# Output tiles one block behind the chain instead of two, and the sample tile in the fifth block

## The chip, the cores and the metric

One Trainium2 chip, one of its cores. A core has TensorE (PE; PEld is its loading of weights), VectorE (DVE), ScalarE (ACT), GpSimd (POOL) and SyncE (SP, which here issues most transfers), each with its own queue of instructions, and 16 DMA engines. The metric is the device time of one execution in microseconds (us).

## The reference

One step of a decoder layer for a prompt of 2048 tokens and a group of 64 sample tokens, with the same weights, 1024 wide:

```python
h = rms_norm(x, norm_pre)
proj = jnp.einsum('btd,de->bte', h, w_in)
...
oc, new_shift, new_S = rwkv7_mix(pc, shift_prev, wkv_S, ...)
...
o = jnp.concatenate([oa, ob, oc, od], axis=-1) * jax.nn.silu(gate)
y = x + rms_norm(jnp.einsum('bte,ed->btd', o, w_out), norm_post)
```

Four groups of heads share the 1024 columns: attention (oa), a gated linear recurrence (ob), RWKV-7 time mixing (oc) and a state space (od). Group C, the RWKV mixing, is a recurrence over the tokens: for each token, `S = S * w + (S @ -kk) (kk * a) + v k` and `y = S r`, for 4 heads with a 64 x 64 state each.

## The kernel before, in words

The input projection, the attention and the groups B and D run first. The last stage, from about 1200 us on, is group C and with it the output projection. Group C goes through the prompt in 16 blocks of 128 tokens, each of two halves of 64 (`rw_prompt`). A block i has these parts:

- the **front** of block i + 2 (`rw_prep`, `rw_mats`, `rw_base`): it depends on the projection alone, not on the state. `rw_prep` makes r_kk, r_W and r_F out of r_X; `rw_mats` multiplies W by F on PE (`ra<-r_W,r_F`), masks the products into r_W and r_ET, and ends with the reduction r_de (L1214). r_de is written to memory (zd) and read back spread out (r_zr); `rw_base` then solves 16 x 16 triangles on VectorE, in 15 pairs of a product (L1262, r_x16w) and a sum (L1263, r_x). The first of them is the row of 128x60 elements;
- **tri** (`rw_tri`): it makes TT of the 16 x 16 inverses by four small products on PE (`rl<-...`);
- the **chain** (`rw_chain`), the recurrence itself, for each half: W times Z on PE, then TT times gs (`rc<-r_gs,r_TT`), which ACT copies into Q, a part of the tile r_Z; BK times Q (`rc<-r_Z,r_BK`), from which VectorE makes the next state (r_Z, L1372); ET times Q (`rc<-r_Z,r_ET`), which ACT copies to r_y;
- the **norm** (`rw_norm`): r_nm, r_yc, r_nss, an inverse square root in small steps (r_nrs), a turn on PE (`rl<-ident,r_yc`), r_yo; and at its end `out_prep`, which multiplies by the gate (o_o), finds a scale by way of o_mx, a 128x1 product on PE (L1550) and the small rows o_q and o_sc, and writes the two halves of o_h (L1561 on ACT, L1562 on VectorE).

`out_tile` is the output projection of 128 tokens: 2 x 24 matmuls of 128 x 512 (L1584), the norm (o_ss, o_y) and the sum with x (o_x, on POOL), which SP stores. There are 16 tiles of the prompt and tile 16 with the 64 sample tokens. A tile's matmuls are laid into the chain of a block: `spine` holds that chain's PE steps, and the k-th group of three matmuls may not start before its share of the steps (`issue_after`). What the loop at L1864 decides is in which block a tile goes out: at block i, tile t goes out if t is at most i - LAG - 1, and LAG is 1. So tile i - 2 is laid into the chain of block i. Tile 16 is prepared in block 15 (`out_prep(16)`) and goes out after tile 14, ahead of tile 15.

The order of the instructions on each engine is then set by a scheduler, which goes through the program with a model of the engines and puts on each what it holds to be ready. An engine works through its order and waits where an operand is missing. Of the pools, o_h and o_x have two buffers, and r_zr has one.

Of the kernel before, what the change touches and what calls it, by code (L numbers as in the profile page):

```python
# [1754 lines left out]
def weave(gens):  # L1755

    gens = [[g, 0, n] for g, n in gens]
    while any(x[2] > 0 for x in gens):
        g = min(gens, key=lambda x: x[1] / abs(x[2]))
        step = next(g[0], 0)  # L1760
        g[1] += 1 if step is None else step
        if step == 0:
            gens.remove(g)


def drain(gen):
    for _ in gen:
        pass


def program(tc, ins, outs):
    with ExitStack() as ctx:
        p = Part(ctx, tc, ins, outs)
        pool = lambda st, name, **kw: st.enter_context(tc.tile_pool(name=name, bufs=1, reuse_waits="tile", **kw))
        nc = tc.nc
        p.attn_consts()
        ph2 = ctx.enter_context(ExitStack())
        with ExitStack() as ph1:
            hp = pool(ph1, "hp", side="right")
            acc = p.pwp = pool(ph1, "acc", space=PSUM, side="right")  # L1780

            def paced(cols, lead):
                pos = -lead
                p.anchors = []

                def after(n):
                    nonlocal pos
                    pos += n
                    i = int(pos * len(p.anchors) / (cols + 1))
                    return p.anchors[min(i, len(p.anchors) - 1)] if pos > 0 else None  # L1790

                return after

            kps = ctx.enter_context(ExitStack())
            kp, sac = pool(kps, "s5k"), pool(kps, "sac")
            with ExitStack() as va:
                vp = pool(va, "vp")
                p.w16b, p.w32b = 8, W32B
                with ExitStack() as st:
                    wp, ps = pool(st, "wp"), pool(st, "stp", space=PSUM)  # L1800
                    lps = pool(st, "lgp", space=PSUM, side="right")
                    sp = wp
                    lr = pool(st, "lr")
                    p.norm_consts(sp)
                    p.wqkv = {0: p.load_w(0, wp, True)}
                    p.norm_in(0, hp, sp, ps)
                    x0, h0 = p.xt_dma, p.hfs[-1]
                    p.qkv_start(wp, vp)
                    for k, b in enumerate(BORD):
                        if k < 4:  # L1810
                            p.norm_in(BORD[k + 1], hp, sp, ps)
                            x1, h1 = p.xt_dma, p.hfs[-1]
                        p.qk(b, sp, acc)
                        with tc.issue_after(x0), tc.issue_after(h0):
                            if k == 0:
                                p.lam_consts(sp, ps)
                                p.lru_consts(sp, ps)
                                p.lru_start(lr)
                            if k == 1:
                                p.proj_dram()  # L1820
                                p.s5_consts(kp, sp)
                            if b == 4:
                                p.sample_consts(sac)
                        if k or LV:
                            p.lru(b, lr, lps, acc)
                        p.vtokens(b, sp, acc)
                        if k == 0 and not LV:
                            p.lru(b, lr, lps, acc)
                        x0, h0 = x1, h1
                p.w16b, p.w32b = W16B, W32C  # L1830
                ev, wp = pool(ph1, "ev", side="right"), pool(ph1, "wp2", side="right")
                aside = p.wo_steps(wp)
                with ExitStack() as st:
                    at, ps = pool(st, "at"), pool(st, "atp", space=PSUM)
                    after = paced(len(FILL) * 2 * TT, LEAD)
                    drain(p.attn_prompt(at, ps))
                    drain(p.proj_rest(FILL, wp, ev, acc, after, aside))
        with kps, ExitStack() as st:
            sp, ps = pool(st, "sa"), pool(st, "sap", space=PSUM)
            weave([(p.attn_sample(sp, ps), SW), (p.s5(pool(st, "s5"), pool(st, "xps", space=PSUM)), S5N)])  # L1840
        with ph2:
            rw, p.late = pool(ph2, "rw", side="right"), pool(ph2, "rwl", side="right")
            p.rps, p.rpb = pool(ph2, "rp", space=PSUM, side="right"), {"ra": 2, "rl": 2, "rc": 2}
            op = pool(ph2, "op")
            with ExitStack() as st:
                p.rwkv_consts(rw)
                seq = p.rw_prompt(rw)
                weave([(p.s5_glu(pool(st, "s5g"), pool(st, "xg", space=PSUM)), 8), (islice(seq, 2 + 4 * RB), RBW)])
            ops = pool(ph2, "ops", space=PSUM)
            p.out_consts(op)  # L1850
            p.opool = pool(ph2, "ot")
            sm = pool(ph2, "sm")
            p.rwkv_sample_consts(sm)
            smp = p.rw_sample(rw, sm)

            def out(t, spine=()):
                if t not in p.prep:
                    p.out_prep(t)
                if GA and t + 1 < 15 and t + 1 not in p.gated and t + 1 not in p.prep:
                    p.out_gate(t + 1)  # L1860
                p.out_tile(t, *p.prep.pop(t), p.opool, ops, spine)

            t = 0
            for i in range(RB, 16):  # L1864
                mark = len(p.spine)
                n = min(-((t - 14) // (16 - i)), i - LAG - t)
                for k in range(4):
                    next(seq, 0)
                    if k in SK:
                        next(smp, 0)  # L1870
                    if n > 0 and k in POSL:
                        out(t, p.spine[mark:])
                        t, n, mark = t + 1, n - 1, len(p.spine)
                    if i == 15 and k == TK:
                        p.out_prep(16)
                while n > 0:
                    out(t)
                    t, n = t + 1, n - 1
            while t < 15:
                out(t)  # L1880
                t += 1
            out(16)
            out(15)


# [11 lines left out]
TK = 1  # L1897
# [21 lines left out]
XTB = 4  # L1919
W16B = 3  # L1920
SSB = 3
LAG = 1
ES = 999
RSP = ()
NAC = 0
# [55 lines left out]
```

## Time and profile before

| | |
|---|---|
| median of 3 runs | 1850.08 us (1841.87 to 1852.64) |
| profiled execution | 1846.33 us |
| its span, first to last instruction | 1844.5 us |
| PE, DVE, ACT, POOL busy | 81%, 79%, 49%, 44% |
| granted PE clock, mean of the span | 0.88 of full speed |

The span is what the profile covers; the profiled execution's own time lies 1.8 us above it. A row of a timeline gives start and duration in us, engine, line, operation, the tile written and those read, the shapes, a count where equal rows follow each other, and in brackets how long the engine stood idle before it and for whom.

### The profile page before, as it was taken

What the parts mean: (1) busy time and instruction counts of PE and PEld (TensorE: products, weight loads), DVE (VectorE), ACT (ScalarE), POOL (GpSimd) and SP (SyncE); (2) the same over time, 40 slices, a digit from 0 to 9 for tenths busy, and PEclk for the clock granted to TensorE, in tenths of its full rate; (3) what the DMA queues carried; (4) which work ended last, traced back from release to release, by engine and by line L of the source; (5) the groups of instructions that cost most, each with busy time, mean ns of one, the idle gap of its engine ahead of it and who ended that gap; (6) DMA issues with size and microseconds to landing.
All of it is one profiled execution on the core that took longest, in us unless ns stands there. A gap on an engine that the chain in (4) does not pass through costs nothing.

```text
span 1844.5 us, 33323 instructions
## 1 busy us (share of the span) xinstructions
PE 1497.3 (81%) x10956; PEld 844.9 (46%) x10956; DVE 1448.1 (79%) x4619; ACT 902.1 (49%) x2211; POOL 811.6 (44%) x887
## 2 busy tenths in 40 slices
PE   4889888987789788878894899657688887887887
PEld 2445644444344344434442456446455454554443
DVE  7797639988899899889896754376878887888865
ACT  3455746655556566657772222243344454444333
POOL 3441326736668877443344454261324333333312
PEclk9999998999899899989996999875777887887889
DMA  4422144575445655464447877635223233333221
GB/s 147 128 91 93 28 116 117 125 149 117 111 111 139 152 141 146 106 145 115 86 104 199 274 250 238 205 96 163 73 66 100 81 105 93 92 86 102 66 72 58
DMA packets 300898, 225.33 MB, mean 122 GB/s; under 512 B 192531, under 2 KB 248565, under 8 KB 300213
## 3 DMA queue, kind: packets, MB, share of 16 engines
q1 hardware_dynamic: 288388, 184.85, 37.4%
q10 hardware_dynamic: 8496, 24.76, 4.7%
q0 software_dynamic: 3840, 13.61, 2.6%
q8 instruction: 86, 1.41, 0.3%
q14 instruction: 88, 0.71, 0.1%
HBM read 130.04 MB, written 53.24 MB: 99 GB/s over the span
## 4 chain that ended last, share of the span: by engine, by line
DVE 34%; PE 21%; DMA 15%; issue 8%; POOL 4%; ACT 3%; SPq 1%; ACTq 0%; POOLq 0%; DVEq 0%
PE acc L206 7%; DMA r_zr<-zd 5%; DVE a_mx L365 4%; PE acc L1584 4%; DVE a_e L389 4%; DMA a_wt<-a_w 3%; DVE r_x L1263 2%; DVE r_x16w L1262 2%; DVE a_w L395 2%; DMA zd<-r_de 2%; PE ss L511 2%; DVE r_W L1177 1%; PE pf L530 1%; POOL a_e L388 1%; POOL a_w L395 1%
## 5 line engine op out<-in xcount | busy, mean ns | idle before, releaser
L206 PE MATMUL acc<-hT,w 128*128 128x512 f16 (+1 forms) x3120 | 633.6, 353 | 24.7 <-ACT pst L640 4.3
L206 PEld LDWEIGHTS <-w 128*128 128x128 f16 x3120 | 269.7, 101 | 322.3 <-issue 66.8
L368 ACT ACTIVATE a_e<-s,a_mx,sig 128x512 f32<-128x512 f32 (+3 forms) x320 | 226.9, 715 | 122.6 <-DVE a_mx L366 106.4
L1584 PE MATMUL acc<-wo,o_h 128*128 128x512 f16 (+1 forms) x816 | 225.1, 422 | 1.2 <-ACT o_y L1588 0.6
L365 DVE TENSOR_REDUCE a_mx<-s 128x1 f32<-128x512 f32 (+3 forms) x320 | 186.3, 599 | 23.4 <-PE s L361 18.7
L388 POOL TENSOR_SCALAR a_e<-a_e,a_al 128x512 f32<-128x512 f32 (+3 forms) x160 | 114.6, 731 | 148.6 <-DVE a_al L384 119.4
L389 DVE SCALAR_TENSOR_TENSOR a_e<-a_e,a_al 128x512 f32<-128x512 f32 (+3 forms) x160 | 149.3, 948 | 9.2 <-POOL a_e L388 9.0
L361 PE MATMUL s<-kh,qh 128*128 128x512 f16 (+3 forms) x320 | 105.7, 359 | 38.2 <-ACT a_e L368 35.0
L402 PE MATMUL pv<-vtok,a_wt 128*128 128x128 f16 x544 | 70.0, 230 | 64.6 <-DMA a_wt<-a_w 57.9
L392 ACT CAST a_w<-a_e 128x512 f16<-128x512 f32 (+3 forms) x160 | 86.3, 557 | 69.9 <-DVE a_e L389 63.5
L1584 PEld LDWEIGHTS <-o_h 128*128 128x128 f16 (+1 forms) x816 | 76.6, 105 | 95.1 <-issue 26.3
L395 POOL TENSOR_TENSOR a_w<-a_e,a_w 128x512 f16<-128x512 f32 (+3 forms) x80 | 90.0, 1128 | 64.4 <-ACT a_w L392 62.4
L1262 DVE TENSOR_TENSOR r_x16w<-r_zr,r_x 128x60 f32<-128x60 f32 (+18 forms) x255 | 58.8, 231 | 67.0 <-DMA r_zr<-zd 63.8
L1599 POOL TENSOR_TENSOR o_x<-o_y,o_x 128x512 f32<-128x512 f32 (+1 forms) x33 | 48.4, 1487 | 121.4 <-DVE o_y L1597 84.7
L402 PEld LDWEIGHTS <-a_wt 128*128 128x128 f16 x544 | 52.2, 104 | 91.4 <-DMA a_wt<-a_w 76.1
L395 DVE TENSOR_TENSOR a_w<-a_e,a_w 128x512 f16<-128x512 f32 (+2 forms) x80 | 76.9, 964 | 2.7 <-ACT a_w L392 2.7
L170 POOL TENSOR_TENSOR hT<-hf,hT 128x512 f16<-128x512 f32 (+1 forms) x36 | 36.5, 1022 | 88.3 <-ACT hT L168 88.2
L403 PE MATMUL pv<-vtok,a_wt 128*128 128x64 f16 x544 | 66.1, 202 | 0.0
L1263 DVE TENSOR_TENSOR r_x<-r_x,r_x16w 128x60 f32<-128x60 f32 (+18 forms) x255 | 62.4, 245 | 3.4
L368 ACT ACTIVATION_READ_ACCUMULATOR a_e<-s,a_mx,sig 128x1 f32 x320 | 64.0, 200 | 0.0
L366 DVE TENSOR_SCALAR a_mx<-a_mx,sig 128x1 f32<-128x1 f32 x320 | 59.8, 201 | 0.4
L511 PE MATMUL ss<-kv,qbd 128*32 128x256 f32 x256 | 52.5, 415 | 6.7 <-DMA kv<-in_ckv 6.5
(552 smaller groups left out, 3378.0 us busy)
## 6 DMA issues: line engine op xcount, KB each, us to landing
kv<-in_ckv SPq DMA_DIRECT2D x128, 256.0 KB
w<-in_w_in ACTq DMA_DIRECT2D x20, 512.0 KB
pc<-pst SPq DMA_DIRECT2D x40, 256.0 KB
xw<-in_xT SPq DMA_DIRECT2D x16, 512.0 KB
w<-in_w_out ACTq DMA_DIRECT2D x16, 512.0 KB
sg<-pst SPq DMA_DIRECT2D x32, 256.0 KB
r_X<-pc SPq DMA_DIRECT2D x16, 512.0 KB
r_zr<-zd SPq DMA_DIRECT2D x16, 512.0 KB
```

Of the source, the lines that this page charges most:

```text
L206: self.nc.tensor.matmul(acc[:, :n], w16[:, k, a, :], h[:, k, e, :], start=(c == 0), stop=(c == 3 * KT - 1))
L361: ins = nc.tensor.matmul(s[:, :kn], q[:, c], kh[:, c, k0:k0 + kn], start=True, stop=True)
L365: nc.vector.tensor_reduce(mx[:, p, c:c + 1], s[:, :kn], axis=AX.X, op=ALU.max, negate=True)
L368: nc.scalar.activation(e[:, :kn], s[:, :kn], AF.Exp, scale=sig, bias=mx[:, p, c:c + 1], accum_out=l[:, p, c:c + 1])
L388: nc.gpsimd.tensor_scalar(e1[:, :kn], e1[:, :kn], al[:, p, 1:2], 0.0, op0=ALU.mult, op1=ALU.add)
L389: nc.vector.scalar_tensor_tensor(e0[:, :kn], e0[:, :kn], al[:, p, 0:1], e1[:, :kn], op0=ALU.mult, op1=ALU.add)
L395: eng.tensor_tensor(w[:, kn:], e0[:, :kn], w[:, :kn], op=ALU.subtract)
L402: ins = nc.tensor.matmul(pv[:, :P], wt[:, j], v, start=kt == 0, stop=kt == qb, skip_group_check=True)
L511: ins = nc.tensor.matmul(sp[g:g + 32, 256 * j:min(256 * j + 256, n)], self.qbd[:, m, s].rearrange("p a q -> p (a q)"), rhs, start=True, st ...
L1262: XV.tensor_tensor(w[:, :, :m], zr[:, k, :, k + 1:], x[:, :, k:k + 1].to_broadcast([P, nu, m]), op=ALU.mult)
L1263: XV.tensor_tensor(x[:, :, k + 1:], x[:, :, k + 1:], w[:, :, :m], op=ALU.add)
L1584: nc.tensor.matmul(a[:n].rearrange("p (c n) -> p c n", c=4), h[:, k, e], self.wo[:, 4 * g:4 * g + 4, k, f, :], start=c == 0, stop=c == 3 * ...
```

## The change

LAG goes from 1 to 0, so tile t may go out in block t + 1: tile i - 1 is laid into the chain of block i. Tile 16 is no longer prepared in block 15 and put out at the end, but prepared and put out in block 4, after the second of the block's four parts. Tiles 14 and 15 stay behind the loop. The instructions of a tile are the same.

```diff
                     if n > 0 and k in POSL:
                         out(t, p.spine[mark:])
                         t, n, mark = t + 1, n - 1, len(p.spine)
-                    if i == 15 and k == TK:
-                        p.out_prep(16)
+                    if i == 4 and k == TK:
+                        out(16)
...
             while t < 15:
                 out(t)
                 t += 1
-            out(16)
             out(15)
...
-LAG = 1
+LAG = 0
```

PE's order in the second half of block 13, of the kernel before. `acc<-wo,o_h` are the output tile's matmuls, `rc` the chain's steps TT, BK and ET; "..." stands for further pairs of the two L1584 rows and, ahead of ET, for two rows of tri and the front and one of the next half.

```order
L44 MATMUL rc<-r_gs,r_TT 64x64 x4
L1584 LDWEIGHTS o_h
L1584 MATMUL acc<-wo,o_h 128x512
...
L44 MATMUL ra<-r_W,r_F 128x128 x8
L44 MATMUL rc<-r_Z,r_BK 64x64 x4
L1584 LDWEIGHTS o_h
L1584 MATMUL acc<-wo,o_h 128x512
...
L44 MATMUL rc<-r_Z,r_ET 64x64 x4
```

Three matmuls of an output tile stand there between TT and BK, and six between BK and ET. The same place on PE in the changed kernel:

```order
L44 MATMUL rc<-r_gs,r_TT 64x64 x4
L1584 LDWEIGHTS o_h
L1584 MATMUL acc<-wo,o_h 128x512
...
L44 MATMUL rc<-r_Z,r_BK 64x64 x4
L1584 LDWEIGHTS o_h
L1584 MATMUL acc<-wo,o_h 128x512
...
L44 MATMUL rc<-r_Z,r_ET 64x64 x4
L1584 LDWEIGHTS o_h
L1584 MATMUL acc<-wo,o_h 128x512
...
L44 MATMUL ra<-r_W,r_F 128x128 x8
```

Now 20 matmuls stand between TT and BK, 22 between BK and ET, and 4 between ET and the front's product W by F, which stood ahead of BK.

VectorE's order at the same place, around the state's row r_Z, in the kernel before:

```order
L1372 TENSOR_TENSOR r_Z<-rc,r_sd 64x128 x2
L1180 TENSOR_TENSOR r_F<-r_kka,r_Di 64x4x64 x2
L1262 TENSOR_TENSOR r_x16w<-r_zr,r_x_20691 128x4x4
L1263 TENSOR_TENSOR r_x_20691<-r_x_20691,r_x16w 128x4x4
L1409 TENSOR_REDUCE r_nm<-r_y 128x4
```

Behind r_Z, which waits for BK, stand r_F and the rows of x16, and then r_nm, which waits for ET. In the changed kernel, the second half of block 13:

```order
L1526 TENSOR_TENSOR o_o<-o_o,o_g 128x768
L1372 TENSOR_TENSOR r_Z<-rc,r_sd 64x128 x2
L1409 TENSOR_REDUCE r_nm<-r_y 128x4
L1413 SCALAR_TENSOR_TENSOR r_yc<-r_nm,r_y 128x256
L1420 TENSOR_REDUCE r_nss<-r_nsq 128x4
```

There r_nm stands directly behind r_Z.

VectorE's order behind the r_de of block 14, in the kernel before, up to the first x16 row; "..." stands for 13 rows, among them r_sv, two rows of tri, r_yc, and the two o_y of an output tile:

```order
L1214 TENSOR_REDUCE r_de<-r_dg 128x64
L111 SCALAR_TENSOR_TENSOR r_nrs<-nq_20927,r_nrs 128x4
...
L1431 TENSOR_TENSOR r_yo<-r_yo,r_sv 128x256
L1152 TENSOR_SCALAR r_ss<-ra 128x4
L1544 TENSOR_TENSOR o_o<-r_yo,o_g_20951 128x256
L1262 TENSOR_TENSOR r_x16w<-r_zr,r_x_21104 128x60
```

The same place in the changed kernel; "..." stands for 5 small rows:

```order
L1214 TENSOR_REDUCE r_de<-r_dg 128x64
L1262 TENSOR_TENSOR r_x16w<-r_zr,r_x_20880 128x4
L111 SCALAR_TENSOR_TENSOR r_nrs<-nq_21116,r_nrs 128x4
L1263 TENSOR_TENSOR r_x_20880<-r_x_20880,r_x16w 128x4
...
L1259 COPY r_x_21706<-eye_15081 128x64
L110 SCALAR_TENSOR_TENSOR nq_21116<-nq_21116,r_nss 128x4
L111 SCALAR_TENSOR_TENSOR r_nrs<-nq_21116,r_nrs 128x4
L1423 TENSOR_TENSOR r_yc<-r_yc,r_nrs 128x256
L1262 TENSOR_TENSOR r_x16w<-r_zr,r_x_21293 128x60
```

The o_y of an output tile, r_yo and o_o no longer stand between r_de and the first x16 row; 18 instructions there have become 12.

## Rows read from the trace of the kernel before

**Rows 1.** The page's first part: busy us, share of the span, instructions.
```profile
PE 1497.3 (81%) x10956; PEld 844.9 (46%) x10956; DVE 1448.1 (79%) x4619; ACT 902.1 (49%) x2211; POOL 811.6 (44%) x887
```

**Rows 2.** The line L1214 in 1310 to 1760 us: durations, first and last start.
```profile
L1214 DVE TENSOR_REDUCE r_de<-r_dg x14: 571/578/593, 1310.2 to 1752.0; 128x64 f32<-128x256 f32 x14
```

**Rows 3.** Busy time by window: length, engines (instructions), granted PE clock, DMA share, GB/s.
```profile
1310.70:1752.60 441.90, 364.45 (x3203) 214.24 (x3203) 366.35 (x1431) 186.05 (x522) 154.67 (x217) 0.81 0.31 87
```

**Rows 4.** Waits of VectorE in 1310 to 1752 us: total us, times, longest.
```profile
DVE r_x16w L1262 <- DMA r_zr<-zd: 53.4, 13, 6.6
DVE o_o L1526 <- DMA o_o<-od: 2.3, 3, 1.0
```

**Rows 5.** Timeline of VectorE behind one r_de: start us, us.
```profile
1687.23 0.58 DVE L1214 TENSOR_REDUCE r_de<-r_dg 128x64 f32<-128x256 f32 x1
...
1694.37 0.16 DVE L99 TENSOR_SCALAR r_rs<-r_ss 128x4 int32<-128x4 int32 x1
1697.61 0.22 DVE L1262 TENSOR_TENSOR r_x16w<-r_zr,r_x 128x60 f32<-128x60 f32 x1 [3.08 <-DMA r_zr<-zd]
```

**Rows 6.** Timeline of SP's queue at the same place.
```profile
1687.83 0.33 SPq L1217 DMA_DIRECT2D zd<-r_de  x1
...
1690.23 0.60 SPq L1221 DMA_DIRECT2D r_zr<-zd  x1
```

**Rows 7.** Timeline of PE in the chain of the last block.
```profile
1785.92 1.06 PE L1584 MATMUL acc<-wo,o_h 128*128 128x512 f16 x3
...
1787.54 2.55 PE L1584 MATMUL acc<-wo,o_h 128*128 128x512 f16 x6
...
1791.64 3.41 PE L1584 MATMUL acc<-wo,o_h 128*128 128x512 f16 x15
1794.98 0.45 PE L44 MATMUL rc<-r_gs,r_TT 64*64 64x64 f32 x8
1795.36 0.82 PE L1584 MATMUL acc<-wo,o_h 128*128 128x512 f16 x3
...
1796.23 0.45 PE L44 MATMUL rc<-r_Z,r_BK 128*64 128x64 f32 x8
1796.61 1.47 PE L1584 MATMUL acc<-wo,o_h 128*128 128x512 f16 x6
1798.01 0.45 PE L44 MATMUL rc<-r_Z,r_ET 64*64 64x64 f32 x8
```

**Rows 8.** Timeline of PE behind an idle time in block 14.
```profile
1763.98 0.66 PE L49 MATMUL rl<-ident,r_yc 128*128 128x128 f32 x2 [5.05 <-DVE o_ss L111]
...
1765.19 1.46 PE L1584 MATMUL acc<-wo,o_h 128*128 128x512 f16 x3
```

**Rows 9.** Timeline of PE at the end: tiles 14, 16 (64 columns) and 15.
```profile
1800.31 5.80 PE L1584 MATMUL acc<-wo,o_h 128*128 128x512 f16 x26 [0.27 <-ACT o_y L1588]
...
1810.71 7.52 PE L1584 MATMUL acc<-wo,o_h 128*64 128x512 f16 x33
1818.16 0.38 PE L1550 MATMUL rl<-o_mx,onec 128*128 128x1 f32 x2
...
1822.73 10.09 PE L1584 MATMUL acc<-wo,o_h 128*128 128x512 f16 x46 [0.29 <-ACT o_y L1588]
```

**Rows 10.** Timeline of VectorE at the end: two rsqrt, first and last row, and o_mx.
```profile
1803.11 0.17 DVE L99 TENSOR_SCALAR r_nrs<-r_nss 128x4 int32<-128x4 int32 x1
...
1808.50 0.15 DVE L111 SCALAR_TENSOR_TENSOR r_nrs<-nq,r_nrs 128x4 f32<-128x4 f32 x1
...
1813.60 0.16 DVE L1548 TENSOR_TENSOR o_mx<-o_mx 128x1 f32<-128x1 f32 x1 [0.64 <-ACT o_j L1547]
...
1834.77 0.15 DVE L99 TENSOR_SCALAR o_ss<-o_ss 128x1 int32<-128x1 int32 x1
...
1836.70 0.16 DVE L111 SCALAR_TENSOR_TENSOR o_ss<-oq,o_ss 128x1 f32<-128x1 f32 x1
```

**Rows 11.** Groups by line in 1310 to 1752 us: busy us, mean ns, idle before.
```profile
L1584 PE MATMUL acc<-wo,o_h 128*128 128x512 f16 x576 | 166.4, 433 | 0.4
```

## The prediction

> **What bounds the kernel now.** I read the page's first part, then the stage that the change touches, by windows, then the waits of VectorE there, then one block in order of time, and the end. Over the whole span PE is the busiest engine, with VectorE close behind [rows 1]; that average says nothing of this stage. The stage is the block loop of group C. Its beat is r_de, the reduction that ends the front of a block: 14 of them lie between 1310.2 and 1752.0 us [rows 2], 13 periods of 34.0 us. In those 441.9 us VectorE works 366.35 and stands idle 75.6 [rows 3]. Of that idle time 53.4 us, in 13 pieces, is the first x16 row waiting for the transfer r_zr<-zd; the next kind of wait makes 2.3 [rows 4]. So a period is 28.2 us of VectorE's work (its 1,431 instructions cost 0.256 us each), 4.1 us of that wait and 1.7 of the rest. PE is busy 364.45 us, but at a granted clock of 0.81, and it does not pace the blocks: VectorE waits for it a few times only.
>
> One block shows why the wait is there. r_de ends at 1687.81; the work that stands behind it in VectorE's order is done by 1694.5, and then VectorE idles 3.08 us until zr has landed at 1697.6 [rows 5]. The two transfers between are issued at 1687.83 and 1690.23 [rows 6]: 9.8 us from r_de to landing. VectorE goes through its rows in order here, so work hides this latency only if it stands between r_de and the first x16 row.
>
> PE puts the output tiles into the chain in small groups: 15 matmuls in 3.41 us between the first half of a block and the second, then 3, then 6 (the last block's rows [rows 7]). That is 0.227 us each. Behind an idle time of 5.05 us, 3 of them take 1.46 [rows 8].
>
> The end: the last chain step is done at 1798.46 [rows 7]; output tiles 14 and 16 fill PE while the last block is normed; the last tile's matmuls start at 1822.73 and take 10.09 [rows 9].
>
> **The change part by part.** Nothing is removed: the same 17 tiles go out, each with 48 matmuls. Tiles 0 to 14 move one block earlier, tile 16 moves from the end into the fifth block. The order shows what follows: a tile's o_h is now ready only late in the chain that it is laid into, so its matmuls no longer stand in groups of 3, 6 and 15 but in runs of 19 to 48.
>
> (a) Work moved ahead of the last r_de. Between the 4th and the last of the 17 r_de rows VectorE has 1,429 instructions before and 1,486 after. 57 more at 0.256 are **+14.6 us**; there is little idle time to hold them, since most of it waits at one fixed row.
>
> (b) The cover of zr's latency. Between r_de and the first x16 row stand, over the 13 blocks, 277 instructions before and 228 after (the order fences show one block: 18 before, 12 now). 49 at 0.256 no longer hide anything: **+12.5 us** of wait. The latency itself I leave at 9.8 us. The SP queue is moved too: in one block the output's store now stands ahead of zd, so that zd waits for the adds on POOL as well; once in 13 blocks, it stays within the range.
>
> [...] The trace measures 9.8, on the hardware queue, so the sum goes by that.
>
> (c) The runs on PE. In 10 of the 13 tiles from 1 to 13 one run of 19 to 48 stands between two steps of a chain, or ahead of tri or the front's matmuls, where there were 3 to 15. In block 13 the second half has 20 between TT and BK and 22 between BK and ET. ACT's copy to Q needs 0.8 us there now at most (BK starts 0.80 us after TT ends, in the last block [rows 7]), so 20 of them, 4.5 us, are not filling but delay. The row of VectorE that waits for BK (r_Z) stands directly ahead of r_nm, which waits for ET: 22 instead of 6 matmuls are 16 x 0.227 = 3.6 us. If each of the 10 costs that, 36 us; if each falls into the wait for zr, which is idle on VectorE anyway, 0. No row of before shows such a run in a block, so these are the bounds. The nearest rows are the other waits of now, which are short [rows 4] with short groups; that speaks for neither bound, and I take the middle, **+18 us**.
>
> (d) The end. Two tiles less stand behind the last r_de. From the last chain step to the last tile's matmuls now pass 24.3 us [rows 7, 9]. Of these, PE's 128x1 product for the last tile waits from 1813.76, when o_mx is done, to 1818.16 behind tile 16's matmuls, 4.4 us [rows 9, 10]; and the rsqrt of the last norm takes 5.5 us from 1803.11 to 1808.65 beside tile 14's, where the very last one, alone, takes 2.1 [rows 10]: 3.4 more. Freed of both: -7.8 us. Against it: the last chain now holds 46 matmuls instead of 33 [rows 7], +3.0 us (13 x 0.227); PE idles some 14 us before the last tile, whose first matmuls then run at half rate, +2 us (about 8 x 0.25 by [rows 7, 8]); and tri of block 15 stands behind all 48 of tile 13, up to 10.5 us, of which I take 3, as x16 hides the rest. Sum **0**, between -8 and +8.
>
> Sum: 14.6 + 12.5 + 18 + 0 = 45 us on the profiled execution's 1846.33 us, **1891 us**. Its median of three is 1850.08, 0.2% above; a difference under 0.5% can't be told from none here. The forecast's own range is 1866 (c at 0, d at -8) to 1918 (c at 36, d at +8).
>
> **The rivals.**
> *It gets faster at the end.* If the runs fall into waits (c at 0), and the 22 us of other idle time swallow the moved work (a at 0), (b) at half leaves 6 us, and the end gives 7.8 and another 7.5, if the last chain is rid of the 33 matmuls in it [rows 7]: 1846 + 6 - 15 = 1837 us. For it speaks that tile 16, 33 of whose 48 matmuls take 7.52 us [rows 9], does leave the end. Against it: PE's order puts 46 matmuls into the last chain. It decides from the point where the periods stay under 35 us.
>
> *It stays the same.* The moved work costs its 14.6 in the blocks, the runs nothing, and the end returns it: 1846 + 14.6 - 7.8 = 1853, within 0.5% of the median. For it: PE has 77 us free in the stage [rows 3]. Against it: VectorE's order decides, not PE's free time.
>
> *PE's clock decides.* A long run comes at full rate: the stage's clock is 0.81 [rows 3], and 3 matmuls after idling cost 0.49 each against 0.227 [rows 7, 8]. The stage's matmuls take 166.4 us, 0.289 each for 576 [rows 11]; at 0.227 they would take 35.7 less. If PE paced the blocks, 1846 + 14.6 - 35.7 = 1825. [...] But PE waits for VectorE here, and the clock gives nothing back.
>
> **How the numbers follow.** The forecast 0.70; slower still, beyond 1920, by a queue or by runs dearer than 3.6 us each, 0.06; the same 0.14; faster at the end 0.07; by the clock 0.03. That makes faster 0.10, same 0.14, slower 0.76. The range from 1842 to 1920 leaves out the dear case and the two fast ones, 0.16.
>
> **What would show it.** Right: r_de's period grows from 34.0 to 36 us and more; the wait of x16 for zr from 53 to some 66 us; new waits of VectorE for PE at r_Z, r_nm or r_W, of 1 us and more; the stretch behind the last r_de stays near 92 us; PE's clock in the stage rises with no gain. Wrong: periods that stay at 34, or an end that shrinks by 15 us or more. Most doubtful is (c), as I read the runs from the order alone: if the copies to Q are late anyway, the runs fill a gap that exists.

## The result

The changed kernel takes 1894.07 us in the median of four runs (1891.1 to 1899.57), the kernel before 1848.68. The ratio is 1.0238, with a 95% interval from 1.0205 to 1.0271. The profiled execution of the changed kernel took 1891.95 us, with a span of 1890.2; that is 45.7 us more than before. Of all executions below one, of the second kernel whose groups are spread over the whole block, ran in a slower state of the chip (2168.52 us at a granted clock of 0.63) and is left out.

The first part of its page, which answers to [rows 1]: over the whole span PE is 22.9 us longer busy and VectorE 1.9, so the 45.7 us are mostly time in which VectorE, the engine that paces this stage, waits.

```profile
PE 1520.2 (80%) x10956; PEld 870.0 (46%) x10956; DVE 1450.0 (77%) x4619; ACT 904.0 (48%) x2211; POOL 819.2 (43%) x887
```

The line of r_de in the block stage (answers to [rows 2]): 13 periods from 1307.2 to 1801.1 us, 38.0 us each, where it was 34.0.

```profile
L1214 DVE TENSOR_REDUCE r_de<-r_dg x14: 542/576/594, 1307.2 to 1801.1; 128x64 f32<-128x256 f32 x14
```

The windows of the stage and of what lies behind it (columns as in [rows 3]):

```profile
1307.20:1801.10 493.90, 401.23 (x3375) 249.30 (x3373) 383.88 (x1487) 199.47 (x557) 166.89 (x221) 0.76 0.28 82
1801.10:1890.20 89.10, 53.01 (x362) 26.44 (x358) 40.04 (x174) 24.04 (x60) 13.48 (x14) 0.76 0.13 45
```

The waits of VectorE in the stage (answer to [rows 4]):

```profile
DVE r_x16w L1262 <- DMA r_zr<-zd: 45.2, 13, 6.6
DVE r_nm L1409 <- ACT r_y L1381: 11.7, 5, 4.9
DVE r_Z L1372 <- PE rc L44: 8.8, 5, 3.6
DVE r_XY L1281 <- POOL r_XY L1270: 4.6, 6, 0.8
DVE o_ss L1592 <- ACT o_j L1590: 4.2, 2, 3.4
DVE r_ss L1152 <- PE ra L44: 4.1, 5, 1.0
```

From these rows the difference of the spans can be put together: the stage begins 3.0 us earlier; VectorE works 17.6 us longer in it (383.88 against 366.25); its wait for zr is 8.2 us shorter (45.2 against 53.4); all its other idle time grows from 22.1 to 64.8 us (493.90 - 383.88 - 45.2), that is +42.7; and the stretch behind the last r_de shrinks from 92.5 to 89.1, -3.4. Together +45.7. The loss is not spread evenly: the three periods that begin at 1519.1, 1671.8 and 1750.3 us are 47.1, 48.3 and 50.8 us long, together 44.2 us over 34.0 each, of the 52.1 that all 13 gain.

In the other idle time the waits at r_nm and r_Z stand first: 11.7 and 8.8 us, where before neither row waited. They are 20.5 of the 42.7 us. The rest is many smaller waits (the rows above, o_ss and r_XY among them) and gaps too short to be listed. Where the waits at r_nm and r_Z come from can be seen in the block that ends the stage. PE, the rows of its second half:

```profile
1782.56 0.69 PE L44 MATMUL rc<-r_gs,r_TT 64*64 64x64 f32 x8
1783.19 5.62 PE L1584 MATMUL acc<-wo,o_h 128*128 128x512 f16 x20
1788.73 0.45 PE L44 MATMUL rc<-r_Z,r_BK 128*64 128x64 f32 x8
1789.12 4.92 PE L1584 MATMUL acc<-wo,o_h 128*128 128x512 f16 x22
1793.97 0.45 PE L44 MATMUL rc<-r_Z,r_ET 64*64 64x64 f32 x8
```

and VectorE at the same time:

```profile
1786.43 1.61 DVE L1526 TENSOR_TENSOR o_o<-o_o,o_g 128x768 f32<-128x768 f32 x1
1789.30 0.59 DVE L1372 TENSOR_TENSOR r_Z<-rc,r_sd 64x128 f32<-64x128 f32 x2 [1.26 <-PE rc L44]
1794.76 0.42 DVE L1409 TENSOR_REDUCE r_nm<-r_y 128x4 f32<-128x256 f32 x1 [4.87 <-ACT r_y L1381]
```

The runs of 20 and 22 that the order showed do stand between TT, BK and ET. They put BK off until 1788.73, so r_Z waits 1.26 us, and ET until 1793.97, so r_nm, directly behind it in VectorE's order, waits 4.87. The page names ACT's r_y for that wait; ACT itself has stood idle for 3.04 us, for PE's ET, when it copies r_y at 1794.46.

### The profile page after: what moved, and what is told of

It is laid out like the page before. It is cut to its first block, busy times and chain, and to the rows that moved or that the text cites. A ratio compares the mean times of both kernels' runs of the same rounds, so it can differ in the third digit from the quotient of the medians.

```text
span 1890.2 us, 33317 instructions
## 1 busy us (share of the span) xinstructions
PE 1520.2 (80%) x10956; PEld 870.0 (46%) x10956; DVE 1450.0 (77%) x4619; ACT 904.0 (48%) x2211; POOL 819.2 (43%) x887
## 4 chain that ended last, share of the span: by engine, by line
DVE 33%; PE 25%; DMA 13%; issue 7%; POOL 5%; ACT 5%; SPq 0%; ACTq 0%; POOLq 0%; DVEq 0%
PE acc L206 7%; PE acc L1584 6%; DMA r_zr<-zd 5%; DVE a_mx L365 4%; DVE a_e L389 3%; DMA a_wt<-a_w 3%; DVE a_w L395 2%; PE ss L511 2%; DVE r_x L1263 2%; DVE r_x16w L1262 2%; PE ra L44 1%; PE pf L530 1%; POOL a_e L388 1%; DVE r_W L1177 1%; PE rc L44 1%
## 5 line engine op out<-in xcount | busy, mean ns | idle before, releaser
L1584 PE MATMUL acc<-wo,o_h 128*128 128x512 f16 (+1 forms) x816 | 212.9, 420 | 11.1 <-ACT o_h L1561 10.3
L1584 PEld LDWEIGHTS <-o_h 128*128 128x128 f16 (+1 forms) x816 | 81.9, 106 | 119.5 <-issue 30.1
L361 PE MATMUL s<-kh,qh 128*128 128x512 f16 (+3 forms) x320 | 105.0, 356 | 37.7 <-ACT a_e L368 34.2
L392 ACT CAST a_w<-a_e 128x512 f16<-128x512 f32 (+3 forms) x160 | 86.3, 557 | 71.4 <-DVE a_e L389 64.9
L395 POOL TENSOR_TENSOR a_w<-a_e,a_w 128x512 f16<-128x512 f32 (+3 forms) x80 | 89.6, 1123 | 62.9 <-ACT a_w L392 60.7
L1588 ACT ACTIVATE o_y<-acc,o_sc 128x512 f32<-128x512 f32 (+1 forms) x34 | 23.3, 687 | 105.3 <-PE acc L1584 105.3
L44 PE MATMUL rc<-r_Z,r_W 128*64 128x64 f32 x512 | 42.2, 289 | 31.5 <-DVE r_Z L1372 31.5
L403 PE MATMUL pv<-vtok,a_wt 128*128 128x64 f16 x544 | 66.6, 202 | 0.0
L1364 POOL TENSOR_TENSOR r_sd<-r_Z,r_Dp 64x128 f32<-64x128 f32 x64 | 30.4, 475 | 76.9 <-DVE r_Z L1372 73.7
```

What stands on the lines that cost most here:

```text
L44: r = self.eng.matmul(*a, **k)
L361: ins = nc.tensor.matmul(s[:, :kn], q[:, c], kh[:, c, k0:k0 + kn], start=True, stop=True)
L392: nc.scalar.copy(w[:, :kn], e0[:, :kn])
L395: eng.tensor_tensor(w[:, kn:], e0[:, :kn], w[:, :kn], op=ALU.subtract)
L1584: nc.tensor.matmul(a[:n].rearrange("p (c n) -> p c n", c=4), h[:, k, e], self.wo[:, 4 * g:4 * g + 4, k, f, :], start=c == 0, stop=c == 3 * ...
```

## The experiments

Theory 1: the runs of output matmuls on PE put off what stands behind them, and VectorE waits for that. Theory 2: the loss comes from o_h being late and VectorE's rows standing in another order, and the runs fill time that is idle anyway. Theory 3: tile 16 upsets the blocks.

The table holds what the views show for each kernel: the ratio to the kernel before, timed beside it, and for the 13 periods of r_de their length, VectorE's busy time, its wait for zr and its other idle time (the length less both), and what lies behind the last r_de, all in us of the profiled execution.

| kernel | median us | ratio (95% interval) | periods | busy | wait for zr | other idle | end |
|---|---|---|---|---|---|---|---|
| before | 1848.68 | 1 | 441.8 | 366.3 | 53.4 | 22.1 | 92.5 |
| changed | 1894.07 | 1.0238 (1.0205 to 1.0271) | 493.9 | 383.9 | 45.2 | 64.8 | 89.1 |
| lag_only | 1880.61 | 1.0182 (1.0137 to 1.0228) | 480.1 | 384.2 | 37.7 | 58.2 | 86.7 |
| s16_only | 1845.25 | 0.998 (0.995 to 1.0011) | 453.7 | 373.1 | 45.3 | 35.3 | 81.2 |
| runs_lag1 | 1889.93 | 1.0216 (1.0178 to 1.0254) | 482.1 | 367.4 | 44.4 | 70.3 | 94.6 |
| run_halves | 1866.9 | 1.0103 (1.0046 to 1.0159) | 459.5 | 374.2 | 35.3 | 50.0 | 98.3 |
| run_behind | 1926.53 | 1.0452 (1.0397 to 1.0506) | 506.7 | 390.4 | 51.2 | 65.1 | 109.1 |
| quarter_before | 1830.01 | 0.9917 (0.9889 to 0.9945) | 441.9 | 367.8 | 40.1 | 34.0 | 82.8 |
| quarter_after | 1854.56 | 1.0043 (1.002 to 1.0066) | 476.6 | 377.6 | 55.1 | 43.9 | 71.1 |
| spread_after | 1926.89 | 1.0431 (1.0404 to 1.0458) | 527.3 | 382.5 | 76.5 | 68.3 | 90.0 |

**The two edits apart.** One kernel has LAG = 0 alone:

```diff
-LAG = 1
+LAG = 0
```

> LAG = 0 alone; tile 16 is prepared in block 15 and goes out at the end, as before. If the runs of output matmuls on PE, and the waits of VectorE for PE behind them, make the loss (theory 1), nearly all of it stays: PE's order has the same runs of 19 to 48. The 57 rows of tile 16 leave the blocks (-15 us) and its matmuls come back to the end (+8 to +12), so about 1885 us, 1870 to 1900, and the periods of r_de grow from 34 to some 36.5 us. If tile 16 in the fifth block makes the loss (theory 3), the time is that of the kernel before, 1840 to 1862.

Measured: 1880.61 us, within that. Some seven tenths of the loss stay, 32 of 45 us.

The other has tile 16 in block 4 alone:

```diff
-                    if i == 15 and k == TK:
-                        p.out_prep(16)
+                    if i == 4 and k == TK:
+                        out(16)
...
-            out(16)
             out(15)
```

> Tile 16 in block 4 alone, LAG = 1. Theory 1: PE's order keeps the groups of 3, 6 and 15, so VectorE pays its 57 rows (+15 us) and one run of 48 (+4), and the end, rid of tile 16, gives back 4 to 15: 1850 us, 1838 to 1866. Theory 3 (the tile upsets the blocks behind it): 1875 us and more, with VectorE's idle time in the stage up by over 20 us.

Measured: 1845.25 us, no difference that can be told. The table shows why: in the blocks 11.9 us are added (6.8 of VectorE's work, the rest waiting), and the end gives back 11.3. Theory 3 falls as the main cause: tile 16's move by itself costs what it brings, and most of the loss is LAG's. Whether the tile costs more on top of LAG = 0 these times leave open, since the intervals of lag_only and of the changed kernel overlap (1.0137 to 1.0228 and 1.0205 to 1.0271).

**The runs alone.** LAG is 1 as before, and o_h as early; only the steps to which the 16 groups are tied are changed, so that they stand as in the worst blocks of the changed kernel:

```diff
-                ins = spine[(KT * g + k) * len(spine) // (2 * KT)] if spine else None
+                ins = spine[len(spine) - 3 + (KT * g + k) // 7] if spine else None
```

> The kernel before with LAG = 1 and tile 16 at the end, but a tile's groups of matmuls are tied to the last three steps of the chain alone: 20 between TT and BK, 22 between BK and ET, 6 behind ET, in every block. o_h is ready as early as before. Theory 1 (a run between the steps of a chain costs by itself): 13 to 15 blocks at some 3.6 us, 1900 us, 1880 to 1925, and VectorE waits for PE at r_Z, r_nm or r_W in most blocks. Theory 2 (the loss comes from o_h being late and from VectorE's rows standing in another order, the runs fill time that is idle anyway): 1845 to 1862.

Measured: 1889.93 us. The rows of one block on PE:

```profile
1700.06 0.69 PE L44 MATMUL rc<-r_gs,r_TT 64*64 64x64 f32 x8
1700.68 6.41 PE L1584 MATMUL acc<-wo,o_h 128*128 128x512 f16 x20
1707.03 0.45 PE L44 MATMUL rc<-r_Z,r_BK 128*64 128x64 f32 x8
1707.41 4.92 PE L1584 MATMUL acc<-wo,o_h 128*128 128x512 f16 x22
1712.26 0.45 PE L44 MATMUL rc<-r_Z,r_ET 64*64 64x64 f32 x8
```

and its stage, by windows and by VectorE's waits:

```profile
1313.60:1795.70 482.10, 380.39 (x3223) 238.05 (x3221) 367.37 (x1446) 189.54 (x528) 148.65 (x217) 0.73 0.28 80
```

```profile
DVE r_x16w L1262 <- DMA r_zr<-zd: 44.4, 13, 5.4
DVE r_nm L1409 <- ACT r_y L1381: 20.7, 11, 4.4
DVE r_nss L1420 <- ACT r_nsq L1419: 15.1, 13, 1.2
DVE r_XY L1281 <- POOL r_XY L1270: 11.4, 12, 1.5
```

VectorE has the work of before (367.4 us); its other idle time grows from 22.1 to 70.3, 3.7 us in each of 13 blocks. The edit alone, with o_h as early as before, so makes a loss as large as that of the whole change. But it acts in two ways. r_nm, which waits for ET behind the runs, waits 20.7 us, in 11 of the blocks. r_nss and r_XY make 26.5 us, where they made 1.6 before, and these wait for ACT and POOL and not for PE. There the order of VectorE's rows has changed too, since the scheduler orders all engines anew for each kernel. In the kernel before x16 rows stand between r_yc and r_nss while ACT makes the squares r_nsq:

```profile
1681.14 0.41 DVE L1413 SCALAR_TENSOR_TENSOR r_yc<-r_nm,r_y 128x256 f32<-128x256 f32 x1
1681.48 0.15 DVE L1262 TENSOR_TENSOR r_x16w<-r_zr,r_x 128x8 f32<-128x8 f32 x1
...
1682.04 0.42 DVE L1420 TENSOR_REDUCE r_nss<-r_nsq 128x4 f32<-128x256 f32 x1
```

In runs_lag1 the x16 rows are done by then, and nothing stands between:

```profile
1713.06 0.42 DVE L1409 TENSOR_REDUCE r_nm<-r_y 128x4 f32<-128x256 f32 x1 [1.43 <-ACT r_y L1381]
1713.51 0.42 DVE L1413 SCALAR_TENSOR_TENSOR r_yc<-r_nm,r_y 128x256 f32<-128x256 f32 x1
1715.17 0.42 DVE L1420 TENSOR_REDUCE r_nss<-r_nsq 128x4 f32<-128x256 f32 x1 [1.24 <-ACT r_nsq L1419]
```

So theory 2 falls as to o_h, which need not be late for the loss; as to the order of VectorE's rows it is not excluded. No run here moves the matmuls and keeps VectorE's order.

**Other places and lengths.** All 48 behind the chain's last step, in one run:

```diff
-                ins = spine[(KT * g + k) * len(spine) // (2 * KT)] if spine else None
+                ins = spine[-1] if spine else None
```

> LAG = 1 again; all 16 groups of a tile are tied to the last step of the chain (ET of the second half), so that the 48 matmuls stand in one run behind the chain, ahead of part of the next chain's W by Z and of tri. If only the place between TT, BK and ET is dear (r_Z and r_nm wait there), this costs little: 1842 to 1862 us. If a run delays whatever stands behind it on PE, 48 matmuls are 10.9 us per block, of which PE's free time (some 6 us per block) hides a part: 5 us in each of 13 blocks, 1910 us, 1885 to 1930.

Measured: 1926.53 us, in the upper part of the second case. The place between TT, BK and ET is not what makes a run dear: behind the chain, where the tri, the norm's turn and the rest of W by Z wait, 48 cost more. Of the 64.9 us that the periods gain 24.1 are VectorE's busy time, with the same number of instructions, 1,433 in the window against 1,431 [rows 3]. Singly the rows do not take longer: their durations add up to 439.9 us here and to 440.2 before. But neighbouring rows of VectorE overlap, by 73.9 us in sum before and by 49.5 here. So VectorE can lose time that no view lists as a wait, with no row longer.

As many matmuls between the steps, in runs of 12 over both halves:

```diff
+                ins = spine[(2, 2, 2, 2, 3, 3, 3, 3, 7, 7, 7, 7, 8, 8, 8, 8)[KT * g + k]] if spine else None
```

> LAG = 1; a tile's groups are tied to W, TT, BK-side steps of both halves alike, so that runs of 12 stand between TT and BK and behind BK in either half: as many matmuls between the steps as with 20, 22 and 6, in shorter runs. If the price is the matmuls beyond ACT's 0.8 us, it is 12 x 0.227 - 0.8 = 1.9 us at each of two r_Z per block: 13 x 3.8 = 49 us at most, some 1885 us, 1870 to 1900. If VectorE has other rows to work on for some 2 us ahead of r_Z and r_nm (a threshold), nearly nothing: 1845 to 1862.

Measured: 1866.9 us, between the two cases. The periods grow by 17.7 us, not by 49. r_Z waits for BK six times, 7.6 us in all, where the sum by the matmuls has a wait at each of 26, so VectorE mostly has other rows for that time. The 17.7 are a balance: 27.9 us of other idle time and 7.9 of work more, and 18.1 less of the wait for zr.

**The same change with short runs.** In both kernels three quarters of each output tile's product are left out, so that a tile has 12 matmuls:

```diff
-            for k in range(KT):
+            for k in range(2):
                 ins = spine[(KT * g + k) * len(spine) // (2 * KT)] if spine else None
...
-                                         start=c == 0, stop=c == 3 * KT - 1)
+                                         start=c == 0, stop=c == 5)
```

> The kernel before with only 2 of the 8 slices of o_h contracted in an output tile: 12 matmuls of a tile instead of 48; the other three quarters of the product are left out. VectorE paces the blocks, so these hardly change (period 34 us); the end loses 36 matmuls of the last tile and those of tiles 14 and 16, some 20 us: 1825 us, 1815 to 1840, by either theory.

> The changed kernel with the same three quarters of each output product left out. Theory 1 (the runs on PE make the loss): runs are 4 to 12 long, and of the 45 us against the kernel before only VectorE's moved rows remain: 5 to 20 us above the other kernel with a quarter, 1838 us. Theory 2 (late o_h and VectorE's order make it): 30 us and more above it, 1855 to 1870.

Measured: 1830.01 and 1854.56 us, 24.6 apart, between what the theories gave (5 to 20, and 30 and more); the profiled execution of the second, in the table, is the longest of its ten. So the loss is about half as large with short runs, and something else is left. The other idle time, which grows by 42.7 us in the full pair, grows by 9.9 here, and the waits at r_nm and r_Z, 20.5 us in the changed kernel, are 1.4. What is left stands mostly in the waits for zr:

```profile
DVE r_x16w L1262 <- DMA r_zr<-zd: 40.1, 13, 5.7
```

of the kernel before with a quarter, and of the changed one with a quarter:

```profile
DVE r_x16w L1262 <- DMA r_zr<-zd: 55.1, 13, 7.7
```

15.0 us of wait are added there, where in the full pair 8.2 are taken away. With short runs the mechanism of term (b), less work of VectorE between r_de and the first x16 row, comes out as forecast. One thing besides the runs' length differs from the full pair: the granted clock of the stage is 0.64 and 0.63, where it was 0.81 and 0.76, and an output matmul takes 0.41 and 0.34 us, where it took 0.289 and 0.257. The short runs last longer than their count says.

**Why the wait for zr was shorter.** In the kernel before, the load of o_g stands half a microsecond ahead of zd on SP's queue in 4 of the 13 blocks. There the turn, from zd to the issue of r_zr, is 3.1 to 4.6 us. One such block, SP's rows:

```profile
1442.03 0.36 SPq L1523 DMA_DIRECT2D o_g<-sg  x1
1442.53 0.45 SPq L1217 DMA_DIRECT2D zd<-r_de  x1
1443.80 0.87 SPq L1117 DMA_DIRECT2D r_xv<-pc  x2
1447.14 0.60 SPq L1221 DMA_DIRECT2D r_zr<-zd  x1
```

r_zr is issued 4.6 us behind zd. In the changed kernel, ahead of the block of 1750.3:

```profile
1748.64 0.36 SPq L1523 DMA_DIRECT2D o_g<-sg  x1
1750.92 0.33 SPq L1217 DMA_DIRECT2D zd<-r_de  x1
1752.43 0.60 SPq L1221 DMA_DIRECT2D r_zr<-zd  x1
```

It is 1.5. VectorE at the same place: 8.2 us from r_de's end to the first x16 row, with only 2.4 us of work between.

```profile
1750.31 0.58 DVE L1214 TENSOR_REDUCE r_de<-r_dg 128x64 f32<-128x256 f32 x1
...
1759.07 0.22 DVE L1262 TENSOR_TENSOR r_x16w<-r_zr,r_x 128x60 f32<-128x60 f32 x1 [5.64 <-DMA r_zr<-zd]
```

Over the 13 blocks the turn from r_de's end to the issue of r_zr is 2.7 us in the mean before and 1.7 after; from there to the first x16 row it is 6.9 and 7.0. To see whether the queue makes it, the gate's loads were given to ACT's queue, in the kernel before:

```diff
-        nc.sync.dma_start(o[:, :6], self.od[b][:, :6, o0:o0 + n])
+        nc.scalar.dma_start(o[:, :6], self.od[b][:, :6, o0:o0 + n])
...
-        nc.sync.dma_start(g, self.sg[b][:, :6, o0:o0 + n])
+        nc.scalar.dma_start(g, self.sg[b][:, :6, o0:o0 + n])
```

> The kernel before, but the loads of o_o and o_g (384 KB each) are issued by ACT's queue and not by SP's, so that SP does not issue the load of o_g 0.5 us ahead of zd in some blocks. If the turn of zd is long (3 to 4.6 us in 4 of 13 blocks) for the sake of those loads' place on SP's queue, the turns from r_de's end to the issue of r_zr fall from 2.7 us in the mean to some 1.7, the wait for zr from 53 to some 44 us and the time by 0 to 10 us: 1840 us. If they are long because the bytes share the 16 DMA engines, whichever queue issues them, nothing changes: 1848 us.

Measured: 1841.92 us, ratio 0.9988 (0.9968 to 1.0008), no difference. The wait for zr is 51.1 us, the turn 2.5 in the mean, and it stays long wherever the load comes close ahead (five blocks, 2.7 to 3.7 us):

```profile
1408.65 0.37 ACTq L1523 DMA_DIRECT2D o_g<-sg  x1
1409.21 0.33 SPq L1217 DMA_DIRECT2D zd<-r_de  x1
1410.16 1.76 SPq L1117 DMA_DIRECT2D r_xv<-pc  x2
1412.95 0.61 SPq L1221 DMA_DIRECT2D r_zr<-zd  x1
```

3.7 us from zd to r_zr, with o_g on another queue. So it is not the place on SP's queue; that the bytes of both meet in the 16 DMA engines fits this but is not shown: one block in gate_act has a turn of 3.3 us with no load near, two in the kernel before have 3.1 and 3.3, and one in the changed kernel has 3.0, so it is not settled.

**The groups spread over the whole block.** The changed kernel, with the groups tied to the later 60% of all PE steps of the block, tri, norm and front among them:

```diff
-                        out(t, p.spine[mark:])
-                        t, n, mark = t + 1, n - 1, len(p.spine)
+                        late = p.PE.done[mark:]
+                        out(t, late[len(late) * 40 // 100:])
+                        t, n = t + 1, n - 1
...
-POSL = (0, 1, 3)
+POSL = (3,)
```

> The changed kernel (LAG = 0, tile 16 in block 4), but a tile's groups are tied not to the ten steps of its chain but to the later 60% of all PE steps of its block, the tri, the norm's turn and the front among them. PE's order then has few runs between TT, BK and ET of the same half; runs of 20 to 24 are left, ahead of W by F and W by Z. If the runs between the chain's steps make most of the loss, it falls to 5 to 20 us: 1850 to 1865 us. If any run of 20 delays what stands behind it, as the run of 48 did in run_behind, 1870 to 1895 us.

> The same with tile 16 at the end: LAG = 0 alone, groups tied to the later 60% of the block's PE steps. By the first theory 1845 to 1862 us (lag_only was 1881), by the second 1865 to 1885.

Measured: 1926.89 us, and 1908.34 us for the second kernel (ratio 1.0309, 1.0268 to 1.0349), slower than either case. Moving most matmuls away from TT, BK and ET does not shrink the loss; but the edit moved more than that, so it does not price the places. The waits of the first:

```profile
DVE r_x16w L1262 <- DMA r_zr<-zd: 76.5, 13, 8.9
DVE r_sv L1243 <- PE ra L44: 8.4, 4, 3.6
DVE r_ss L1152 <- PE ra L44: 5.8, 3, 2.8
```

Here both kinds of waiting add up: 131 instructions of VectorE are left between r_de and the first x16 row over the 13 blocks (277 before), and the wait for zr is 23.1 us longer; the other idle time is up by 46.2, with runs of 20 to 24 ahead of tri, the norm's turn or the front in six blocks. Runs of 9 to 13 between the chain's steps are left in most blocks, and the block with tile 16 has runs of 44 and 33 there and a period of 54.7 us.

**A better place for tile 16.** In block 1, where no other tile goes out, tied to that block's chain, and the same with the gate's loads on ACT's queue:

```diff
-                    if i == 15 and k == TK:
-                        p.out_prep(16)
+                    if i == 1 and k == TK:
+                        out(16, p.spine[-10:])
```

> LAG = 1; tile 16 goes out in block 1, in which no prompt tile goes out, tied to that block's chain. One run of 44 is left instead of those of 48 and 23 in block 4, whose period in s16_only was 51.6 us. If that period came from the runs beside another tile's groups, some 8 us come back: 1837 us, 1828 to 1846. If the period pays VectorE's rows for tile 16 alone, the same as s16_only, 1845 us.

> Both: tile 16 in block 1, and the gate's loads issued by ACT. If the two add up, 1830 us, 1820 to 1842; if not, as the better of the two.

Measured: 1845.2 us (ratio 1.0002, 0.998 to 1.0023) and 1856.39 us (1.0073, 1.0043 to 1.0103). Neither is faster than the kernel before. In the first the periods grow by 9.6 us and the end gives back 4.9, so the 8 us that might have come back did not. The second lies above both of its cases (1820 to 1842, or as the better of the two); why was not pursued.

## Why the prediction was right, and where its terms were not

The forecast was 1891 us on the profiled execution; this is 1891.95. The forecast of slower held, with moved work and waits behind runs on PE as causes. That the sum came within a microsecond is luck: the four terms came out at +17.6, -8.2, +42.7 and -3.4 where +14.6, +12.5, +18 and 0 were forecast, and the stage begins 3.0 us earlier, for which there was no term. (Added up from its terms the forecast's own range is 1865.4 to 1917.4, not 1866 to 1918.)

**(a) Moved work**, forecast +14.6 us; measured +17.6 of busy time. Right, with 56 instructions more in the windows (1,487 against 1,431 [rows 3]): the durations of VectorE's rows add up to 12.0 us more, and 5.7 come from rows that overlap less. Not all of it is tile 16: with LAG = 0 alone VectorE's busy time grows by as much (384.2), with tile 16 alone by 6.8.

**(b) The cover of zr's latency**, forecast +12.5 us; measured -8.2. This step failed, at "The latency itself I leave at 9.8 us", and its other side was priced too high. The 49 instructions are gone (277 against 228), but they hid little: between r_de and the first x16 row VectorE is busy 60.7 us over the 13 blocks where it was 66.6, so the cover shrank by 5.9 us, not by 12.5. The latency, from r_de's end to that row, went from 124.7 to 113.4 us, 9.6 to 8.7 each, and other idle time within it from 4.7 to 7.5. 5.9 less 11.3 less 2.8 is the -8.2. The shorter latency goes along with loads of the gate that no longer stand close ahead of zd; that they make it is not shown. A forecast that left one side of the difference alone could not see it. The pair with a quarter, where the latency stays (121.4 and 119.7) and the cover shrinks by 18.0 us, gives +15.0. In no block of either kernel does the work in the gap cover the latency: it is 1.3 to 6.6 us long where 8.2 to 11.0 us pass from r_de's end to the first x16 row.

**(c) The runs on PE**, forecast +18 us between 0 and 36; measured +42.7, if all other idle time is put down to it. The two waits that it priced, r_Z for BK and r_nm for ET, came to 20.5 us; that runs on PE can cause them is seen in runs_lag1, and that they go with the runs' length in the pair with a quarter. The other 22.2 us are waits that no term had: o_ss, r_XY, r_ss, r_nss and more, of which the views do not say how much is due to the runs. The term was so mis-sized, at "that speaks for neither bound, and I take the middle". Nor is the loss 3.6 us in each of ten blocks: three periods hold 44.2 of the 52.1 us. In each of the three two runs of 10 to 22 stand between the steps of its second half, rows behind r_nm wait there too, and VectorE idles 16 to 18 us. The block of 1605.9 us, with runs of 14 and 22, has a period of only 35.5: VectorE has 96 rows and 27.3 us of work in it, where the three have 119 to 124 rows and 30.7 to 33.3 us, and idles 8.2. Why it idles less is open.

**(d) The end**, forecast 0 between -8 and +8; measured -3.4. The rows of PE:

```profile
1853.83 0.45 PE L44 MATMUL rc<-r_Z,r_ET 64*64 64x64 f32 x8
...
1862.67 0.59 PE L1550 MATMUL rl<-o_mx,onec 128*128 128x1 f32 x2 [2.61 <-DVE o_mx L1548]
1865.85 12.97 PE L1584 MATMUL acc<-wo,o_h 128*128 128x512 f16 x48 [2.60 <-ACT o_h L1561]
```

From the last chain step to the last tile now pass 11.6 us where it was 24.3 [rows 7, 9]: 12.7 given back, 5 more than the 7.8 forecast. The last tile, behind idle time, takes 12.97 us for 48 matmuls where the row of before has 10.09 for 46; +2 were forecast, from "about 8" at half rate, a count that no row of before shows. Here 12 of them start 0.42 us apart and the rest 0.215, some 2.5 us. From the last r_de to the last chain step it is 53.2 us where it was 46.5, +6.7, where 6 were forecast for tile 13 ahead of tri and the 46 matmuls in the last chain.

**The rivals.** Faster at the end fell because the periods grew to 38.0 us, above its 35. The same fell because the runs cost. PE's clock decides fell twice over: PE does not pace the blocks, and the granted clock of the stage did not rise, which the prediction too had expected, but fell from 0.81 to 0.76. The output matmuls themselves did get faster, 0.257 us each (170.3 for 662) where it was 0.289 [rows 11], without gain. Nor did keeping matmuls together bring a higher clock in the other kernels with long runs: runs_lag1 and run_behind have granted clocks of 0.73 and 0.68 in the stage and are slower.

## What to carry to other kernels

Work that is off the critical path, laid into a chain on an engine that goes through its order in turn, can put off the chain's steps: here runs of 20 and 22 made r_Z wait 1.26 us and r_nm 4.87 in one block. Look at how many instructions stand between two steps of the chain, multiply by the row's duration, and name who waits. Here such work, moved closer to its producer, came late, and what was 3 and 6 became 20 and 22. And for a covered latency forecast both sides, the cover and the latency, from each block's rows, since the same change may move both. Count a cover in busy time and not in rows, as rows can overlap: by 73.9 us in sum in the 13 periods of the kernel before. And where a scheduler orders all engines, compare the waiting engine's order before and after: here no edit to PE's matmuls left VectorE's rows in their order.

## What was not expected of the hardware

Long runs on PE went with a lower mean clock: it is 0.76 in the stage of the changed kernel, 0.73 in runs_lag1 and 0.68 in run_behind, where it was 0.81. In runs_lag1 the granted clock is 0.50 from 1690 to 1700 us, where PE is busy 5.3 of 10 us; TT takes 0.69 us there. It is 0.69 in the mean over the 20 matmuls behind it, which take 6.41 us, 0.32 each, and 1.00 over the next 22, which take 4.92, 0.224 each; BK between them takes 0.45. So the clock rose within a run, and the first run took some 1.9 us more for it (an estimate: 6.41 less 20 x 0.224). In the block that ends the stage of the changed kernel it is 0.50 over TT, which takes 0.69 us there too, and up to 1785.5 us, 2.3 us into the run of 20, and 1.00 from there to the end of the run of 22: 5.62 us for the 20, 4.92 for the 22. Runs are not the only way to a low clock: with three quarters of the output matmuls left out, in runs of 6 and less, the stage is at 0.64.

A load of 384 KB issued 0.5 to 0.8 us ahead of a 32 KB store went with a longer turn of the store, 2.7 to 4.6 us where 1.5 is the shortest, on the same queue (up to 4.6) as on another (up to 3.7). Four turns of 3.0 to 3.3 us in the same three kernels had no such load near, so the cause is open.

Neighbouring rows of VectorE overlap in the trace. In the 13 periods of the kernel before, the rows' durations add up to 440.2 us and fill 366.3. In run_behind nearly the same rows add up to 439.9 us and fill 390.4.
